# Half-height score products, splits of whole tiles and paired stores in a two-layer encoder on one core

## The chip, the cores and the metric

The kernel runs on one core of one Trainium2 chip. The metric is the device time of one execution in microseconds (us). The kernel before takes 1310.69 us, the median of 3 runs (1310.45 to 1311.05). About 0.2% (2.6 us) is the least difference that a measurement of this kernel can tell from none.

## The reference

Two encoder layers over 512 tokens of width 1024 in f32, and a final RMSNorm. Each layer adds three blocks to x: neighbourhood attention beside grouped-query attention with one output projection, attention over 256 memory tokens, and a gated feed-forward block with a convolution over positions. Only the grouped-query scores and the final norm matter here:

```
def gqa_block_attention(q, k, v):          # 8 query heads, 2 key heads, head width 64
    qb = q.reshape(b, nblk, Q_BLOCK, hkv, g, dh).transpose(1, 0, 2, 3, 4, 5)
    ...
        sc = jnp.einsum('bqkgd,bskd->bkgqs', qi, k, preferred_element_type=jnp.float32) * scale
        p = jax.nn.softmax(sc, axis=-1)
        return jnp.einsum('bkgqs,bskd->bqkgd', p.astype(v.dtype), v)
...
    return rms_norm(x, norm_final)
```

A query block is 128 tokens, and the sum over d in a score runs over 64 values.

## The kernel before

**Arithmetic.** Products are taken on TensorE in a rounded f32 type (F32R). To keep f32 accuracy each operand is split into a rounded part (hi) and what is left (lo): ACT casts hi, DVE or POOL subtracts lo. A full product is three products into one PSUM buffer, hi by hi, hi by lo, lo by hi (`mm3`, line 635).

**Layout.** x stands transposed in eight tiles xT of 128 rows of the model width by 512 tokens, one tile each (line 647). PSUM has buffers with three tags: mm (4), sc (2) and tr (2), each 128 x 512 f32.

**Grouped-query attention** (lines 1094 to 1269). `gqa_project_kv` and `gqa_project_q` project, normalise and turn k and q, and transpose them on TensorE, so that in the transposed tile the rows 0 to 63 belong to one key head and the rows 64 to 127 to the other. `split_k` (line 958) writes for each head j a tile gk[j] whose 128 rows hold that head's k twice: the head's 64 rows are cast and subtracted over 64 partitions, and a DMA (line 971) copies them to the other 64. `split_q` (line 976) writes q for head j with its hi on 64 rows and its lo on the other 64. With the rows stacked so, one product over 128 rows gives hi and lo of q at once, and `gqa_scores` (line 1206) needs two products for each head: q by hi of k and q by lo of k, both into that head's sc buffer. A unit u is one block of 128 queries and one pair of heads (j = 0, 1), so it has 4 products of 512 columns; 16 units a layer, 32 in all. Behind the products come the row maximum and its scaling on DVE, the exponential on ACT (which reads the sc buffer last), normalisation on POOL, transposes and the product with v.

**The order.** Nothing is issued where the code calls it. `Tape` records each call as a `Step` with a cost (`times`, line 125), and `plan` simulates the engines and chooses an order for each. On PE it takes, among up to 300 steps ahead, the first in the recorded order that can start within 60 ns of the earliest one; a step that opens a PSUM buffer can only start when a buffer of that tag is free. `play` (line 387) then issues all steps in the planned order. So every instruction in the profile has line 395, the call in `play`, and groups are told apart by tile names.

**The end** (`down_last`, line 1633). The last feed-forward product leaves 384 token columns in the layout of xT (output 0) and the last 128 tokens the other way round, as two halves of 512 model columns in two sc buffers (output 1). `squares` sums their squares on ACT and multiplies them by the norm's gains on DVE. The eight chunks of xT are scaled on DVE (five) and POOL (1, 4 and 6), and SP stores each by itself. Then 640 columns of the last 128 tokens are scaled by the root on DVE and stored by SP, 384 on ACT and stored from ACT's queue.

Of the kernel before, what the change touches and what calls it, by code (L numbers as in the profile page):

```python
# [11 lines left out]
F32 = mybir.dt.float32  # L12
F32R = mybir.dt.float32r
AF = mybir.ActivationFunctionType
ALU = mybir.AluOpType
# [4 lines left out]
P = 128  # L20
S = 512
D = 1024
# [4 lines left out]
KC = D // P  # L27
# [64 lines left out]
class Step:  # L92
# [32 lines left out]
    def times(self):  # L125

        n = max(columns(a) for a in (self.writes if self.engine == E_PE else self.reads + self.writes))
        if self.engine == E_PE:
            busy = max(110.0, (n + 32) / 2.4)
            if self.reads[0].dtype == F32 and self.name != "transpose" and "is_transpose" not in self.call[2]:  # L130
                busy = 222.0
            return busy, busy + 170.0
        narrow = min(a.ap[0][1] for a in self.writes) < P
        if self.engine == E_ACT:
            busy = 68.0 + 0.805 * n if any(tag_of(a.tensor) in IN_PSUM for a in self.reads) else 85.0 + 0.855 * n
            busy += 105.0 * (n > 1) * sum(columns(a) == 1 for a in self.reads) + 93.0 * (len(self.writes) > 1)
            return busy + 110.0 * narrow, busy + 105.0 + 100.0 * (len(self.writes) > 1)
        wide = sum(columns(a) > 16 for a in self.reads)
        if self.engine == E_DVE:
            if self.name == "tensor_tensor_reduce":  # L140
                return 382.0, 540.0
            busy = 64.0 + 1.05 * n
            if n <= 16:
                busy = 130.0
            elif self.name in ("tensor_scalar", "scalar_tensor_tensor"):
                busy = 120.0 + 1.05 * n if wide > 1 else 64.0 + 0.78 * n
            return busy, busy + 85.0
        if self.name in ("tensor_scalar", "tensor_copy"):
            busy = 245.0 + 0.82 * n
        else:  # L150
            busy = 480.0 + 145.0 * n if tag_of(self.reads[-1].tensor) == "mhalf" else 120.0 + 2.2 * n
        return busy, busy + 45.0
# [337 lines left out]
def encoder_kernel(ctx: ExitStack, tc: tile.TileContext, t: dict, out: list):  # L490
# [21 lines left out]
    def rtile(shape, dt=F32R):  # L512
        return rpool.tile([P, *shape], dt, tag="r", name=nm("r"), padded_shape=[P, *pad(shape)])
# [15 lines left out]
    def small(n):  # L529
        return spool.tile([P, n], F32, tag="s", name=nm("s"), padded_shape=[P, 16])  # L530
# [7 lines left out]
    f = lambda ap: ap.bitcast(F32)  # L538
# [105 lines left out]
            mm3(ps, wh[:, k, c], wl[:, k, c], *ops[k], k == first, k == last)  # L644


    xg0 = [xpool.tile([P, S + 1], F32, tag=f"x{c}", name=f"xT{c}") for c in range(KC)]
    xT = [x[:, 0:S] for x in xg0]
    par = cpool.tile([P, DEPTH, NPAR], F32, name="par")
    first = nc.const_aps.tensor(0.0, (P, P), F32)  # L650
# [240 lines left out]
    for l in range(DEPTH):  # L891
# [66 lines left out]
        def split_k(pm, kt, near):  # L958
            rows = [(slice(64 * j, 64 * j + 64), slice(64 - 64 * j, 128 - 64 * j)) for j in range(2)]
            for k, (r, o) in zip(kt, rows):  # L960
                ACT.copy(k[r, 0], pm[r])
                if near:
                    ACT.copy(k[o, 0], pm[r])
            for k, (r, o) in zip(kt, rows):
                DVE.tensor_sub(k[r, 1], pm[r], f(k[r, 0]))
                if near:
                    DVE.tensor_sub(k[o, 1], pm[r], f(k[r, 0]))

            def double():
                for k, (r, o) in zip(kt, rows):  # L970
                    SP.dma_start(f(k[o]), f(k[r]))

            if not near:
                double()
# [167 lines left out]
        def gqa_project_kv():  # L1142

            w = [get_w(("gkv", kh), AHEAD - kh) for kh in range(2)]
            keys, gv = [], rtile((NB, 2, P))
            for m in range(2):
                pm = ps_mm().rearrange("p (b c) -> p b c", b=2)
                for i in range(2):
                    bs = slice((2 * m + i) * P, (2 * m + i + 1) * P)
                    for k in range(KC):  # L1150
                        wh, wl = (v[:, k % 4, :] for v in w[k // 4])
                        mm3(pm[:, i], xg[k][0][:, bs], xg[k][1][:, bs], wh, wl, k == 0, k == KC - 1)
                        if k == 3 or k == KC - 1 and i == 0:
                            yield
                x = pm[:, :, 0:P].rearrange("p b (h d) -> p b h d", d=HD)
                b = slice(2 * m, 2 * m + 2)
                r = head_norm(x, 4, 1, b)
                for i in range(2):
                    gvt[2 * m + i] = gv[:, 2 * m + i]
                    split_psum(gvt[2 * m + i][:, :, 0:HD], gvt[2 * m + i][:, :, HD:P],  # L1160
                               pm[:, i, P:].rearrange("p (h d) -> p h d", d=HD), mix.rstd[:, 2 * m + i : 2 * m + i + 1])
                tk = tmp((2, P))
                turned(x, 4, 1, b, tk.rearrange("p b (h d) -> p b h d", d=HD))
                heads = tk.rearrange("p b (h d) -> p (b h) d", d=HD)
                POOL.tensor_mul(heads, heads, r.unsqueeze(2).to_broadcast([P, 4, HD]))
                keys.append(tk)
                yield

            def turn():
                tr = ps_t()  # L1170
                for b in range(NB):
                    PE.transpose(tr[:, b * P : (b + 1) * P], keys[b // 2][:, b % 2], ident)
                gk.extend(rtile((2, S)) for _ in range(2))
                split_k(tr, gk, False)

            late(2, turn)

# [18 lines left out]
        def gqa_turn_q(b, tq):  # L1196
            tr = ps_t()
            for i in range(4):
                PE.transpose(tr[:, i * P : (i + 1) * P], tq[:, i * P : (i + 1) * P], ident)
            gq[b] = rtile((2, 4, P))  # L1200
            split_q(tr.rearrange("p (i n) -> p i n", i=4), gq[b])


        ga, gpt = {}, {}
# [1 line left out]
        def gqa_scores(u):  # L1206
            i, b = divmod(u, NB)
            sc = [ps_s() for _ in range(2)]
            for j in range(2):
                for part in range(2):  # L1210
                    PE.matmul(sc[j], gq[b][:, j, i], gk[j][:, part], start=part == 0, stop=part == 1)
            nmx, sums = small(2), small(2)
            es = []
            for j in range(2):
                c, h = slice(j, j + 1), slice(2 * i + j, 2 * i + j + 1)
                DVE.tensor_reduce(nmx[:, c], sc[j], axis=AX.X, op=ALU.max, negate=True)
                DVE.tensor_scalar(nmx[:, c], nmx[:, c], gr[b][:, h], 1.0, op0=ALU.mult, op1=ALU.mult)
                e = tmp()
                ACT.activation(e, sc[j], AF.Exp, bias=nmx[:, c], scale=gr[b][:, h], accum_out=sums[:, c])
                es.append(e)  # L1220
            ga[u] = es, sums
# [411 lines left out]
        def down_last(j0, nj):  # L1633
# [41 lines left out]
            def squares(i):  # L1675
                sq = tmp()
                ACT.activation(sq, pms[i], AF.Square, accum_out=sums[:, i : i + 1])
                DVE.tensor_mul(y[:, i], pms[i], gains[:, 512 * i : 512 * i + 512])

            for i in range(2):  # L1680
                pms.append(ps_s())
                for c in range(4):
                    PE.matmul(pms[i][:, c * P : (c + 1) * P], xT[4 * i + c][:, tail], ident, start=c == 0, stop=False,
                              is_transpose=True)
                closing(i, range(2))
                if i == 0:
                    norm.stat()
                    closing(i, range(2, nj))
                    squares(i)
            part0, dev, rstd = small(1), small(1), small(1)  # L1690
            DVE.tensor_scalar(part0, sums[:, 0:1], 1.0 / D, EPS, op0=ALU.mult, op1=ALU.add)
            norm.spread()
            for k in range(KC):
                xk = xT[k][:, cs]
                if k in (1, 4, 6):
                    POOL.tensor_mul(xk, xk, norm.rep)
                else:
                    DVE.tensor_mul(xk, xk, norm.psum)
                SP.dma_start(out[0][k * P : (k + 1) * P, :], xk)
            closing(1, range(2, nj))  # L1700
            ACT.activation(small(1), sums[:, 0:1], AF.Sqrt)
            squares(1)
            ACT.activation(dev, sums[:, 1:2], AF.Sqrt, bias=part0, scale=1.0 / D)
            DVE.reciprocal(rstd, dev)
            yf = y.rearrange("p i n -> p (i n)")
            DVE.tensor_scalar(yf[:, :640], yf[:, :640], rstd, 1.0, op0=ALU.mult, op1=ALU.mult)
            SP.dma_start(out[1][:, 0:640], yf[:, :640])
            ACT.activation(yf[:, 640:], yf[:, 640:], AF.Copy, scale=rstd)
            ACT.dma_start(out[1][:, 640:D], yf[:, 640:])

        for n in range(NF):
            if n == 0:
# [164 lines left out]
```

## Time and profile before

| | us |
|---|---|
| median of 3 runs | 1310.69 |
| the profiled execution's own time | 1310.14 |
| its span, first to last instruction | 1308.0 |
| PE busy | 1299.9 |
| weight loads (PEld) busy, beside PE | 1121.9 |
| DVE / POOL / ACT busy | 1057.7 / 808.5 / 738.4 |

The granted TensorE clock has a mean of 0.998. In the rows of groups, "out<-in" are tile names, "128*128" behind PE is rows by columns of the array that the product uses, "128x512" the output, then the count; behind the bar stand busy us in total, mean ns of one, and the engine's idle time just before them with what ended it. A product's recorded duration reaches beyond the start of the next one, since products are pipelined; the spacing of starts is what each adds. The tiles in rows: r are operands in SBUF, sc, mm and tr are PSUM buffers, xT is x.

### The profile page before, as it was taken

What the parts mean: (1) busy time and instruction counts of PE and PEld (TensorE: products, weight loads), DVE (VectorE), ACT (ScalarE), POOL (GpSimd) and SP (SyncE); (2) the same over time, 40 slices, a digit from 0 to 9 for tenths busy, and PEclk for the clock granted to TensorE, in tenths of its full rate; (3) what the DMA queues carried; (4) which work ended last, traced back from release to release, by engine and by line L of the source; (5) the groups of instructions that cost most, each with busy time, mean ns of one, the idle gap of its engine ahead of it and who ended that gap; (6) DMA issues with size and microseconds to landing.
All of it is one profiled execution on the core that took longest, in us unless ns stands there. A gap on an engine that the chain in (4) does not pass through costs nothing.

```text
span 1308.0 us, 19584 instructions
## 1 busy us (share of the span) xinstructions
PE 1299.9 (99%) x6937; PEld 1121.9 (86%) x6937; DVE 1057.7 (81%) x2008; ACT 738.4 (56%) x1391; POOL 808.5 (62%) x607
## 2 busy tenths in 40 slices
PE   9999999999999999999999999999999999999997
PEld 8898888888888888888888988888888888888897
DVE  7679986766999998987545898956769999989865
ACT  7777686555445544544537767865645445444442
POOL 4465867627667677773726657774466667776651
PEclk9999999999999999999999999999999999999999
DMA  8742313313323333332365422233133333333321
GB/s 283 218 146 51 111 49 97 97 38 118 91 79 115 109 97 97 99 116 92 105 161 178 128 67 81 65 113 82 49 113 97 98 97 100 110 95 99 99 95 65
DMA packets 42673, 137.41 MB, mean 105 GB/s; under 512 B 5072, under 2 KB 8656, under 8 KB 42576
## 3 DMA queue, kind: packets, MB, share of 16 engines
q1 hardware_dynamic: 42144, 135.83, 34.6%
q8 instruction: 55, 0.90, 0.3%
q14 instruction: 42, 0.34, 0.1%
q10 hardware_dynamic: 432, 0.33, 0.1%
HBM read 126.18 MB, written 2.10 MB: 98 GB/s over the span
## 4 chain that ended last, share of the span: by engine, by line
PE 99%; DMA 1%; DVE 0%; ACT 0%; SPq 0%; issue 0%
PE mm L395 52%; PE sc L395 25%; PE tr L395 22%; DMA xT<-in_w 0%; DMA r<-in_w 0%; DVE xT L395 0%; ACT xg L395 0%; ACT r L395 0%; DVE tr L395 0%; DVE r L395 0%; ACT rep L395 0%; SPq L395 0%; ACT hi L395 0%; DVE s L395 0%
## 5 line engine op out<-in xcount | busy, mean ns | idle before, releaser
L395 POOL TENSOR_TENSOR lo<-raw,hi 128x512 fp32r<-128x512 f32 (+2 forms) x236 | 438.2, 1868 | 305.9 <-ACT hi L395 305.0
L395 ACT CAST hi<-raw 128x512 fp32r<-128x512 f32 (+2 forms) x276 | 219.9, 817 | 186.7 <-PE sc L395 70.8
L395 PE MATMUL mm<-r,hi 128*128 128x512 f32 (+2 forms) x928 | 247.1, 346 | 0.0
L395 PE MATMUL sc<-xg,hi 128*128 128x512 f32 (+1 forms) x740 | 229.0, 391 | 0.2 <-ACT hi L395 0.2
L395 PE MATMUL tr<-xg,hi 128*128 128x512 f32 x672 | 207.1, 389 | 0.0
L395 PEld LDWEIGHTS mm<-r,hi 128*128 128x128 f32 x928 | 163.2, 189 | 21.8
L395 PE MATMUL mm<-r,lo 128*128 128x256 f32 (+2 forms) x496 | 165.6, 334 | 0.0
L395 PEld LDWEIGHTS sc<-xg,hi 128*128 128x128 f32 x740 | 137.2, 189 | 27.3 <-ACT hi L395 0.6
L395 PE MATMUL mm<-r,r 128*128 128x256 f32 (+2 forms) x1040 | 158.4, 293 | 0.0
L395 PEld LDWEIGHTS tr<-xg,hi 128*128 128x128 f32 x672 | 126.0, 188 | 26.1
L395 PEld LDWEIGHTS mm<-r,r 128*128 128x128 f32 x1040 | 142.4, 191 | 2.7
L395 POOL TENSOR_TENSOR r<-t,r 128x512 fp32r<-128x512 f32 x80 | 117.9, 1478 | 42.5 <-ACT r L395 42.2
L395 PE MATMUL sc<-xg,lo 128*128 128x512 f32 (+1 forms) x370 | 143.5, 389 | 0.0
L395 ACT CAST r<-t 128x512 fp32r<-128x512 f32 (+1 forms) x164 | 94.4, 588 | 85.2 <-DVE t L395 68.7
L395 PE MATMUL tr<-xg,lo 128*128 128x512 f32 x336 | 130.7, 389 | 0.0
L395 DVE TENSOR_TENSOR xT<-xT,mm 128x256 f32<-128x256 f32 (+2 forms) x216 | 116.6, 559 | 15.8 <-PE mm L395 9.5
L395 PE MATMUL mm<-xg,hi 128*128 128x512 f32 (+1 forms) x386 | 121.7, 394 | 0.0
L395 DVE TENSOR_TENSOR t<-t,t 128x512 f32<-128x512 f32 (+2 forms) x110 | 116.5, 1079 | 5.5 <-ACT t L395 2.9
L395 PE MATMUL mm<-hi,xg 128*128 128x512 f32 (+1 forms) x384 | 108.5, 358 | 0.0
L395 POOL TENSOR_SCALAR t<-t,s 128x512 f32<-128x512 f32 (+1 forms) x112 | 67.2, 614 | 63.5 <-DVE s L395 57.6
L395 PEld LDWEIGHTS mm<-r,lo 128*128 128x128 f32 x496 | 93.9, 189 | 9.5
L395 DVE TENSOR_TENSOR r<-t,r 128x512 fp32r<-128x512 f32 (+1 forms) x84 | 81.6, 992 | 8.3 <-ACT r L395 7.6
(138 smaller groups left out, 2421.9 us busy)
## 6 DMA issues: line engine op xcount, KB each, us to landing
raw<-in_w SPq DMA_DIRECT2D x207, 512.0 KB, 3.7
r<-r SPq DMA_DIRECT2D x30, 256.0 KB, 3.6
r<-in_bias SPq DMA_DIRECT2D x16, 384.0 KB, 4.8
raw<-in_w SPq DMA_DIRECT2D x8, 384.0 KB, 3.0
r<-in_memT SPq DMA_DIRECT2D x4, 512.0 KB, 6.7
xT<-in_w SPq DMA_DIRECT2D x7, 256.5 KB, 4.5
out<-xT SPq DMA_DIRECT2D x8, 192.0 KB, 2.0
r<-in_w SPq DMA_DIRECT2D x9, 128.0 KB, 4.3
```

What stands on the lines that cost most here:

```text
L395: call(*args, **kwargs)
```

## The change

1. Scores: each head takes three products over its own 64 rows (hi by hi, hi by lo, lo by hi) in place of two over 128 rows, recorded alternately for the two heads, so that rows 0 to 63 and 64 to 127 follow each other.
2. q and k are split as the transpose left them: one cast and one subtraction over 128 partitions for both heads. The DMA that doubles k is gone, and so is one of the two k tiles of a layer.
3. The planner prices a product over fewer than 128 rows at half, plus 6 ns.
4. xT tiles are allocated in pairs, and the final store takes a pair: four stores of two chunks in place of eight of one.
5. The second half row is no longer multiplied by the gains ahead of the root; one DVE instruction multiplies it from PSUM by root and gains. The split of the last scaling goes from 640 and 384 columns to 512 and 512.

```diff
@@ Step.times
                 busy = 222.0
+            if self.reads[0].shape[0] < P:
+                return busy / 2 + 6.0, busy + 170.0
             return busy, busy + 170.0
@@ x's tiles
-    xg0 = [xpool.tile([P, S + 1], F32, tag=f"x{c}", name=f"xT{c}") for c in range(KC)]
+    xpair = [xpool.tile([P, 2, S + 1], F32, tag=f"x{c}", name=f"xT{c}") for c in range(KC // 2)]
+    xg0 = [xpair[c // 2][:, c % 2] for c in range(KC)]
@@ turn (k), gqa_turn_q
-                gk.extend(rtile((2, S)) for _ in range(2))
-                split_k(tr, gk, False)
+                gk.append(rtile((2, S)))
+                split_psum(gk[0][:, 0], gk[0][:, 1], tr)
...
-            split_q(tr.rearrange("p (i n) -> p i n", i=4), gq[b])
+            split_psum(gq[b][:, 0], gq[b][:, 1], tr.rearrange("p (i n) -> p i n", i=4))
@@ gqa_scores
-            for j in range(2):
-                for part in range(2):
-                    PE.matmul(sc[j], gq[b][:, j, i], gk[j][:, part], start=part == 0, stop=part == 1)
+            for n, (a, c) in enumerate(((0, 0), (0, 1), (1, 0))):
+                for j in range(2):
+                    r = slice(64 * j, 64 * j + 64)
+                    PE.matmul(sc[j], gq[b][r, a, i], gk[0][r, c], start=n == 0, stop=n == 2)
@@ down_last
                 ACT.activation(sq, pms[i], AF.Square, accum_out=sums[:, i : i + 1])
-                DVE.tensor_mul(y[:, i], pms[i], gains[:, 512 * i : 512 * i + 512])
...
                     squares(i)
+                    DVE.tensor_mul(y[:, 0], pms[0], gains[:, :512])
...
-                SP.dma_start(out[0][k * P : (k + 1) * P, :], xk)
+                if k % 2:
+                    SP.dma_start(out[0][(k - 1) * P : (k + 1) * P].rearrange("(i p) c -> p i c", p=P), xpair[k // 2][:, :, cs])
...
-            yf = y.rearrange("p i n -> p (i n)")
-            DVE.tensor_scalar(yf[:, :640], yf[:, :640], rstd, 1.0, op0=ALU.mult, op1=ALU.mult)
-            SP.dma_start(out[1][:, 0:640], yf[:, :640])
-            ACT.activation(yf[:, 640:], yf[:, 640:], AF.Copy, scale=rstd)
-            ACT.dma_start(out[1][:, 640:D], yf[:, 640:])
+            DVE.scalar_tensor_tensor(y[:, 1], pms[1], rstd, gains[:, 512:], op0=ALU.mult, op1=ALU.mult)
+            SP.dma_start(out[1][:, 512:], y[:, 1])
+            ACT.activation(y[:, 0], y[:, 0], AF.Copy, scale=rstd)
+            ACT.dma_start(out[1][:, :512], y[:, 0])
```

The planned order on PE, at the first two units of layer 0, in the kernel before (sc_401 and sc_402 are the buffers of the first unit's two heads, sc_411 and sc_412 those of the second's; r_350 and r_351 are the two heads' k):

```order
L395 MATMUL sc_401<-r_350,r_362 128x512 x2
L395 MATMUL sc_402<-r_351,r_362 128x512 x2
L395 MATMUL mm_410<-r_232,hi_391 128x512 x2
L395 MATMUL mm_410<-r_232,lo_392 128x512
L395 MATMUL mm_410<-r_284,hi_391 128x512 x2
L395 MATMUL mm_410<-r_284,lo_392 128x512
L395 MATMUL mm_410<-r_337,hi_391 128x512 x2
L395 MATMUL mm_410<-r_337,lo_392 128x512
L395 MATMUL mm_410<-r_372,hi_391 128x512 x2
L395 MATMUL mm_410<-r_372,lo_392 128x512
L395 MATMUL sc_411<-r_350,r_379 128x512 x2
L395 MATMUL mm_417<-r_232,hi_391 128x512
```

The same two units after the change (sc_396 and sc_397, then sc_406 and sc_407; r_346 holds both heads' k):

```order
L397 MATMUL sc_396<-r_346,r_357 128x512
L397 MATMUL sc_397<-r_346,r_357 128x512
L397 MATMUL sc_396<-r_346,r_357 128x512
L397 MATMUL sc_397<-r_346,r_357 128x512
L397 MATMUL sc_396<-r_346,r_357 128x512
L397 MATMUL sc_397<-r_346,r_357 128x512
L397 MATMUL mm_405<-r_228,hi_386 128x512 x2
...
L397 MATMUL sc_406<-r_346,r_374 128x512 x3
L397 MATMUL mm_412<-r_228,hi_386 128x512 x2
L397 MATMUL mm_412<-r_228,lo_387 128x512
L397 MATMUL sc_407<-r_346,r_374 128x512 x3
```

The first unit's six products alternate between the heads. The second unit's stand in two groups of three, one for each head, with three products of the output projection between. In all, 26 of the 32 units stand like the second, 3 like the first, and 3 in between.

At the end of the program, SP's last instructions before the change (xT_76 to xT_83 are the eight chunks, r_2389 the last 128 tokens):

```order
L395 DMA out<-xT_76 128x384
L395 DMA out<-xT_77 128x384
L395 DMA out<-xT_78 128x384
L395 DMA out<-xT_79 128x384
L395 DMA out<-xT_80 128x384
L395 DMA out<-xT_81 128x384
L395 DMA out<-xT_82 128x384
L395 DMA out<-xT_83 128x384
L395 DMA out<-r_2389 128x640
```

And after it (xT_76 to xT_79 are the four pairs):

```order
L397 DMA out<-xT_76 128x2x384
L397 DMA out<-xT_77 128x2x384
L397 DMA out<-xT_78 128x2x384
L397 DMA out<-xT_79 128x2x384
L397 DMA out<-r_2383 128x512
```

Nine stores became five. The first store of before waits for DVE alone, which scales chunk 0; the first of after waits for DVE and for POOL, which scales chunk 1.

## The prediction

> **What bounds the kernel now.** I read the page first: busy time by engine, then the chain of work that ended last. After it come the waits of PE alone, and pieces of the chain in order of time.
>
> ```profile
> span 1308.0 us, 19584 instructions
> PE 1299.9 (99%) x6937; PEld 1121.9 (86%) x6937; DVE 1057.7 (81%) x2008; ACT 738.4 (56%) x1391; POOL 808.5 (62%) x607
> ...
> PE 99%; DMA 1%; DVE 0%; ACT 0%; SPq 0%; issue 0%
> ```
>
> ```profile
> PE tr L395 <- PEq L1869: 0.8, 1, 0.8
> PE sc L395 <- ACT hi L395: 0.2, 1, 0.2
> ```
>
> ```profile
> 465.57 5.47 PE sc L395 x24
> ...
> 663.85 21.88 PE mm L395 x96
> ```
>
> PE is busy for 1299.9 of 1308.0 us, the chain is PE for 99%, and in the whole span PE waits 1.0 us for anybody. So time is what PE's instructions cost, one behind the other, and a few us at the end. An instruction's price on this chain is not its recorded duration but its spacing: 5.47 us for 24 products of 512 columns is 228 ns each, and 21.88 us for 96 is 228 ns again. The stage that the change rewrites must be looked at by itself, so I asked for busy time by engine from the first to the last group of grouped-query scores in each layer (columns: length, then PE, weight loads, DVE, ACT, POOL).
>
> ```profile
> 135.90:202.00 66.10, 66.10 (x361) 55.65 (x360) 60.73 (x132) 52.31 (x113) 50.21 (x53) 1.00 0.25 73
> 781.00:858.00 77.00, 76.95 (x420) 64.51 (x419) 69.30 (x149) 60.78 (x130) 55.91 (x59) 1.00 0.24 73
> ```
>
> PE is busy for 66.10 of 66.10 us and for 76.95 of 77.00; DVE comes next with 60.73 and 69.30. Here too PE alone decides, at a granted clock of 1.00.
>
> **Scores: what a product of 64 rows costs.** There are 32 units (2 layers of 16), one each for a query block and a pair of heads. Before, a unit has 4 products over 128 rows: 4 x 228 = 912 ns. After, it has 6 over 64 rows. The trace has none over 64 rows; the nearest rows are the groups of products with shapes kept apart (last two numbers ahead of the bar's end: busy us, mean ns).
>
> ```profile
> L395 PE MATMUL sc<-xg,hi 128*128 128x512 f32 x732 | 226.4, 390 | 0.2 <-ACT hi L395 0.2
> ...
> L395 PE MATMUL sc<-r,r 128*128 128x256 f32 x224 | 33.7, 285 | 0.0
> ...
> L395 PE MATMUL mm<-r,r 128*128 128x384 f32 x96 | 17.3, 334 | 0.0
> ```
>
> From 256 to 384 to 512 columns the mean goes 285, 334, 390 ns: the price follows the columns that stream through, about 0.4 ns each. Rows are 128 in every row of this trace, so their effect is not shown. Bounds for one 64-row product of 512 columns: half, 114 ns, if price went with the share of the array in use, and 228 ns if it goes with columns alone. I take 228, since columns explain all three rows. Then the half array that is left unused pays only if the other head's product runs in it at the same time. For such a pair the bounds are 228 ns (wholly beside) and 456 ns (one behind the other); I take 228, as two products over separate rows and separate PSUM buffers share neither.
>
> So all hangs on which products stand next to each other, and there the order of the change decides. Its rows above show the first unit alternating between the two heads (sc_396, sc_397), six products in a row. The next shows three products of one head (sc_406 x3), three products over 128 rows, and then three of the other head (sc_407 x3). I went through all 32 units in the order:
>
> - 3 units alternate cleanly. Each costs 3 x 228 instead of 4 x 228 ns: 3 x -0.23 = -0.7 us.
> - 3 are broken in part (one product alone, then five alternating, twice; and once two of each head, then one of each). Each fills 4 slots of 228 ns, as before: 0.
> - 26 have all three products of one head, then 1 to 10 products of other work over 128 rows, then all three of the other. Three products on the same 64 rows cannot stand beside each other, and the next on PE needs all rows. Each costs 6 x 228 instead of 4 x 228 ns, +0.456 us: 26 x 0.456 = +11.9 us.
>
> The sum is **+11.2 us**, all of it on PE, which the chain runs through. The Trainium skill, "TensorE: Matmul & The Clock Gate", Part 3 (The mechanism), states that matmuls in different row groups start about 4 ns apart, and that matmuls start and end strictly in program order; by the first the pair costs 232 ns, and by the second a head's three products cannot move across the others to find a partner. No run yet shows the first.
>
> **Splits of q and k.** With the head's two halves left where the transpose puts them, 20 casts and 20 subtractions over 64 partitions become 10 and 10 over 128, and 4 copies of k (r<-r) leave SP's queue.
>
> ```profile
> L395 DVE TENSOR_TENSOR r<-tr,r 128x512 fp32r<-128x512 f32 x48 | 32.4, 685 | 10.8 <-ACT r L395 10.5
> ...
> L395 DVE TENSOR_TENSOR r<-tr,r 64x512 fp32r<-64x512 f32 x20 | 13.8, 689 | 0.7 <-issue 0.2
> L395 ACT CAST r<-tr 64x512 fp32r<-64x512 f32 x20 | 11.6, 579 | 6.9 <-PE tr L395 6.6
> ```
>
> Sixty-four or 128 partitions cost the same (689 and 685 ns), so DVE saves 10 x 0.69 = 6.9 us and ACT 10 x 0.58 = 5.8 us. On the path that is worth nothing: PE hides it, since it never waits for a split in the two stages. If that cover went (PE faster by 7.3 us over two stages, the best case), DVE would still have 60.73 - 3.4 = 57.3 us of work in a stage of 62.4. Between 0 and -0.2 us, the one wait for ACT that there is; I take 0. The planner lays out the whole program anew, but instruction counts by kind are otherwise the same, and it counts on scores that are done sooner than I expect, so what waits for PE has more time than planned: 0, up to +1 us if one hand-over goes wrong.
>
> **The end.** Stores of x's rows now go in pairs, and the last half row is multiplied straight from PSUM. I read the last 9 us in order of time, each engine by itself, and then the DMA rate (last column, GB/s) in short stretches.
>
> ```profile
> 1299.49 2.41 DVE L395 TENSOR_TENSOR xT<-xT,tr 128x384 f32<-128x384 f32 x5 [0.54 <-ACT rep L395]
> 1299.53 1.01 POOL L395 TENSOR_TENSOR xT<-xT,rep 128x384 f32<-128x384 f32 x1 [2.97 <-ACT rep L395]
> ...
> 1300.07 0.34 SPq L395 DMA_DIRECT2D out<-xT  x1
> ...
> 1300.58 0.85 SPq L395 DMA_DIRECT2D out<-xT  x2
> ...
> 1301.82 0.69 DVE L395 TENSOR_TENSOR r<-sc,r 128x512 f32<-128x512 f32 x1
> ...
> 1304.02 0.60 SPq L395 DMA_DIRECT2D out<-r  x1
> ```
>
> ```profile
> 1300.60:1300.80 0.20, 0.20 (x2) 0.00 (x0) 0.20 (x1) 0.00 (x0) 0.20 (x1) 1.00 0.00 0
> 1300.80:1301.00 0.20, 0.11 (x1) 0.00 (x0) 0.20 (x2) 0.06 (x1) 0.20 (x1) 1.00 0.36 131
> 1301.00:1301.20 0.20, 0.00 (x0) 0.00 (x0) 0.20 (x1) 0.20 (x1) 0.20 (x1) 1.00 1.04 376
> ...
> 1306.25:1306.50 0.25, 0.00 (x0) 0.00 (x0) 0.00 (x0) 0.00 (x0) 0.00 (x0) 0.50 0.98 369
> 1306.50:1306.75 0.25, 0.00 (x0) 0.00 (x0) 0.00 (x0) 0.00 (x0) 0.00 (x0) 0.50 0.11 31
> ```
>
> From 1300.9 to 1306.5 us the DMA engines are full, at about 375 GB/s. The removed DVE multiply (0.69 us) and the last store, which now comes some 1 us sooner on SP, stand beside this and bring nothing. What sets the end is when the first byte leaves and how many there are. The bytes are the same (8 x 192 + 320 + 192 KB before, 4 x 384 + 2 x 256 after). The first store left at 1300.07, when DVE had its chunk; after, it needs POOL's chunk too, which ends at 1299.53 + 1.01 = 1300.54, and in the trace the second store, which waits for that, leaves at 1300.58. So everything starts 0.5 us later: **+0.5 us**, with 0 if larger stores move faster and +0.7 if they take longer to issue.
>
> **Sum.** The profiled execution took 1310.14 us, and + 11.2 + 0.5 makes 1321.8. The median of the three runs, 1310.69, lies 0.55 above that execution; I forecast against it: **1322.4 us**.
>
> **Rivals.**
>
> *Half price (faster).* A 64-row product costs its half whatever stands next to it, 114 ns. Then a unit costs 684 instead of 912 ns: 32 x -0.228 = -7.3, +0.5 at the end: 1303.9 us. It decides wherever the price of a product lies under 912 / 6 = 152 ns. For it: no row here varies the number of rows, and in the new order each head's three products share their moving and stationary buffers. Against it: columns alone explain the means at 256, 384 and 512. Chance 0.11. A price close to 152 would give no change: 0.03.
>
> *Every change of rows empties the array.* The recorded 390 ns of a product, less its spacing of 228, leaves about 161 ns in which a product is still under way while the next streams. If PE must be empty before it goes from 128 rows to 64 or back, each change costs up to that. The 32 units stand in 60 unbroken runs of 64-row products, thus 120 changes: up to 120 x 0.161 = +19.3 us, 1341.7 us. The Trainium skill, "TensorEngine Tiling (Array Packing)", Key Properties, says that a change of tiling mode drains the TensorE, while another tile in the same mode does not; all groups here are 128*128, so nothing in this trace shows it. For it: 60 runs is an order that would suffer most. Against it speaks the nearest change of kind that PE makes now, from transposes to products and back, in order of time.
>
> ```profile
> 142.72 0.60 PE L395 MATMUL tr<-ident,t 128*128 128x128 f32 x4
> 143.07 0.48 PE L395 MATMUL mm<-r,hi 128*128 128x512 f32 x1
> 143.39 0.60 PE L395 MATMUL tr<-ident,t 128*128 128x128 f32 x4
> 143.74 1.18 PE L395 MATMUL sc<-r,r 128*128 128x512 f32 x4
> 144.76 0.39 PE L395 MATMUL mm<-r,hi 128*128 128x512 f32 x1
> ```
>
> Eight transposes and five products take 2.04 us from 142.72 to 144.76; less 5 x 0.228 that is 112 ns for a transpose of 128 columns, and no room for four changes at 0.16. I give a cost that is well visible (over 8 us) 0.20, and let smaller ones stand within the forecast, whose own range is 1318 to 1330: 0.62.
>
> *Weight loads come to light.*
>
> ```profile
> L395 PEld LDWEIGHTS sc<-r,r 128*128 128x128 f32 x376 | 57.6, 189 | 5.8 <-DMA r<-r 0.2
> ```
>
> If loads onto the same 64 rows did not run beside products there, up to 189 ns for each of the 192 products, 36 us more: 1358 us. Against it, PEld is busy for 1121.9 us beside PE's 1299.9, all of it on the same rows. Chance 0.04.
>
> **How the numbers follow.** Forecast 0.62, emptied array 0.20, loads 0.04, half price 0.11, no change 0.03. The range takes in the first two: 1316 to 1344. About 0.2% (2.6 us) is what a measurement of this kernel can tell from no change; so faster 0.11, same 0.03, slower 0.86.
>
> **What the changed profile would show.** Products marked by 64 rows: 192 of them, spaced by 228 ns within a run of three, and two that start within a few ns in the 3 clean units. Stages of about 66.1 + 5.0 and 77.0 + 6.2 us (12 and 14 whole units at 0.456, less 2 and 1 x 0.228). A spacing near 114 in runs of three makes me wrong towards faster; a gap at each first product of a run, or behind its last, makes the second rival right. At the end, a first store near 1300.6 on the old clock, and DMA full for 5.6 us behind it. PE waiting for DVE or ACT in these stages would say that the new plan, not the products, is at work.

## The result, and the profile after

The changed kernel takes 1346.21 us (median of 4 runs, 1344.84 to 1347.60), the kernel before beside it 1310.87 (4 runs, 1310.45 to 1312.35): a ratio of 1.027, 95% interval 1.0256 to 1.0281. It is 35.3 us slower. Slower was forecast; the time lies 2.2 us above the range.

The page after, and the waits of PE:

```profile
span 1344.5 us, 19676 instructions
PE 1335.2 (99%) x7001; PEld 1125.6 (84%) x7001; DVE 1051.5 (78%) x1997; ACT 733.0 (55%) x1381; POOL 807.2 (60%) x607
```

```profile
PE tr L397 <- PEq L1873: 0.8, 1, 0.8
PE sc L397 <- DMA r<-r: 0.4, 1, 0.4
PE sc L397 <- DVE xg L397: 0.2, 1, 0.2
```

PE still waits for nobody (1.4 us in all) and is busy 35.3 us longer; DVE and ACT are busy 6.2 and 5.4 us less; the splits were to save them 6.9 and 5.8. To divide the loss between the stream on PE and the end, take the last eleven products of both programs (line 397 is line 395 of before), the store of the first chunk, and the span. Before:

```profile
1298.16 2.75 PE L395 MATMUL sc<-r,r 128*128 128x512 f32 x11
1298.98 0.48 ACT L395 COPY rep<-tr 128x384 f32<-128x384 f32 x1 [0.62 <-DVE tr L395]
1300.07 3.86 SPq L395 DMA_DIRECT2D out<-xT  x8
```

After:

```profile
1333.98 2.77 PE L397 MATMUL sc<-r,r 128*128 128x512 f32 x11
1334.80 0.48 ACT L397 COPY rep<-tr 128x384 f32<-128x384 f32 x1 [0.61 <-DVE tr L397]
1336.40 2.59 SPq L397 DMA_DIRECT2D out<-xT  x4
1338.78 0.35 ACTq L397 DMA_DIRECT2D out<-r  x1
1339.08 0.90 SPq L397 DMA_DIRECT2D out<-r  x1
```

The last products start 35.82 us later; from there to the end of the span it was 9.84 us and is 10.52: +0.7 at the end. Of the 35.8 us, 11.2 were forecast. The other 24.6 can be seen where the units stand. This is PE in order of time at the first two units (start, length, then the group):

```profile
135.95 0.60 PE L397 MATMUL tr<-ident,t 128*128 128x128 f32 x4
136.47 0.96 PE L397 MATMUL sc<-r,r 64*128 64x512 f32 x6
137.37 0.73 PE L397 MATMUL mm<-r,hi 128*128 128x512 f32 x2
137.94 0.39 PE L397 MATMUL mm<-r,lo 128*128 128x512 f32 x1
...
139.98 0.39 PE L397 MATMUL mm<-r,lo 128*128 128x512 f32 x1
140.30 0.96 PE L397 MATMUL sc<-r,r 64*128 64x512 f32 x3
141.19 0.73 PE L397 MATMUL mm<-r,hi 128*128 128x512 f32 x2
141.76 0.39 PE L397 MATMUL mm<-r,lo 128*128 128x512 f32 x1
```

Six products that alternate between the heads last as long (0.96) as three of one head: pairs do run side by side. But from 139.98 to 141.76 six products start, each 228 ns, 1.37 us together, and 1.78 us pass: the run of three costs 0.41 us more than its products. The 192 products stand in 60 unbroken runs (52 of three, the others of one, five or six). If each pays the same, that is 60 x 0.41 = 24.6 us, all that was missing. The weight loads of the same place show what happens there:

```profile
139.76 0.19 PEld L397 LDWEIGHTS mm<-r,lo 128*128 128x128 f32 x1
140.30 0.52 PEld L397 LDWEIGHTS sc<-r,r 64*128 64x128 f32 x3 [0.35 <-ACT t L397]
141.19 0.30 PEld L397 LDWEIGHTS mm<-r,hi 128*128 128x128 f32 x2 [0.37 <-issue]
```

Within work of one kind a load runs ahead, beside the product before it (the load at 139.76 is for the product at 139.98). At a change from 128 rows to 64, and at the change back, the load starts only 0.32 us after the last product's start (139.98 to 140.30, 140.87 to 141.19), some 0.09 later than the next product would have started. The next product's start is recorded at the same moment as its load, and the second product of a run starts 0.335 us after the first instead of 0.228; we read this as a first product that is held up by its own load, which costs 0.11. Together 0.20 us a change, twice a run. The name in the brackets misleads: the trace puts the first gap down to ACT, whose first exponential over the first unit had ended at 139.30, and the second to "issue". But at all 58 changes from a run back to a product over 128 rows the gap is 0.315 to 0.324 us, whatever the profile names.

### The profile page after: what moved, and what is told of

It is laid out like the page before. It is cut to its first block, busy times and chain, and to the rows that moved or that the text cites. A ratio compares the mean times of both kernels' runs of the same rounds, so it can differ in the third digit from the quotient of the medians.

```text
span 1344.5 us, 19676 instructions
## 1 busy us (share of the span) xinstructions
PE 1335.2 (99%) x7001; PEld 1125.6 (84%) x7001; DVE 1051.5 (78%) x1997; ACT 733.0 (55%) x1381; POOL 807.2 (60%) x607
## 4 chain that ended last, share of the span: by engine, by line
PE 98%; DVE 1%; DMA 1%; ACT 0%; issue 0%; DVEq 0%
PE mm L397 51%; PE sc L397 26%; PE tr L397 21%; DMA r<-r 1%; ACT t L397 0%; DVE t L397 0%; ACT r L397 0%; DVE sc L397 0%; DVE s L397 0%; DVE r L397 0%; ACT hi L397 0%; DVE mm L397 0%; DVE xT L397 0%; DVE xg L397 0%; ACT s L397 0%
## 5 line engine op out<-in xcount | busy, mean ns | idle before, releaser
L397 PE MATMUL mm<-r,hi 128*128 128x512 f32 (+2 forms) x928 | 250.8, 349 | 0.0
L397 PE MATMUL sc<-r,r 128*128 128x256 f32 (+2 forms) x440 | 96.7, 353 | 0.4 <-DMA r<-r 0.4
```

What stands on the lines that cost most here:

```text
L397: call(*args, **kwargs)
```

## The experiments

Three theories went in. **A**: each change of PE between 128 and 64 rows costs 0.20 us, and products cost a slot of 228 ns each, shared by two on different halves. **B**: 64-row products are dear by themselves. **C**: the new order of the program costs the time. The kernel before, beside these runs, took 1310.73 us for the first four, 1311.18 for the next three and 1310.54 for the last two.

**All rows, same order.** The price stays at half by a flag, so that the planned order on PE is the same, product for product.

```diff
-                    r = slice(64 * j, 64 * j + 64)
-                    PE.matmul(sc[j], gq[b][r, a, i], gk[0][r, c], start=n == 0, stop=n == 2)
+                    PE.matmul(sc[j], gq[b][:, a, i], gk[0][:, c], start=n == 0, stop=n == 2)
```

> The changed kernel with its six products a unit taken over all 128 rows of the tiles in place of 64, in the same order of instructions on PE (so the scores sum both heads, and the output is not the reference's). It changes nothing but the number of rows. Theory A (each change of PE between 128 and 64 rows costs about 0.20 us, 120 of them): the changes are gone, and 192 products cost 228 ns where 128 did, +14.6 us, with +0.6 at the end: 1326 us. Theory B (every 64-row product is dear by itself, 0.11 us more than one of 128 rows, because its weight load comes to light): 1326 us too. Theory C (the new order, made with a price of half a product, costs the time): 1340 us or more, since the order stays.

1325.68 us, a ratio of 1.0115 (1.010 to 1.013). The order alone costs nothing, C is out: with it and without changes of rows the sum of products (+14.6) and the end (+0.6) account for the time. The changed kernel, with the same products in the same order on PE, takes 20.5 us more although 16 pairs save it a slot each (3.6 us). That is 24.2 us for 120 changes, 0.20 each; theory B could still claim them for the 192 products. The same place as above:

```profile
139.84 0.39 PE L400 MATMUL mm<-r,lo 128*128 128x512 f32 x1
140.07 0.84 PE L400 MATMUL sc<-r,r 128*128 128x512 f32 x3
140.75 0.62 PE L400 MATMUL mm<-r,hi 128*128 128x512 f32 x2
141.20 0.39 PE L400 MATMUL mm<-r,lo 128*128 128x512 f32 x1
```

The same six products take 1.36 us from 139.84 to 141.20, against 1.78 with 64 rows.

**Pairs without anything between.** The six products are one step for the planner, with a price of 1089 ns. (The planner's rule for free buffers is extended, since such a step opens two.)

```diff
-            for n, (a, c) in enumerate(((0, 0), (0, 1), (1, 0))):
-                for j in range(2):
-                    r = slice(64 * j, 64 * j + 64)
-                    PE.matmul(sc[j], gq[b][r, a, i], gk[0][r, c], start=n == 0, stop=n == 2)
+            def scores(sc0, accum_out, qh, ql, kh, kl):
+                for n, j in [(n, j) for n in range(3) for j in range(2)]:
+                    r = slice(64 * j, 64 * j + 64)
+                    q, k = ((qh, kh), (qh, kl), (ql, kh))[n]
+                    nc.tensor.matmul((sc0, accum_out)[j], q[r], k[r], start=n == 0, stop=n == 2)
+            tape.take(E_PE, "scores", scores, (sc[0],), {"accum_out": sc[1], ...})
```

> The changed kernel with the six products of a unit issued as one block that alternates between the heads, so that none of the planned work comes between them: 32 runs of 64-row products in place of 60, all of them paired. Theory A: each unit costs 3 slots of 228 ns plus two changes, 1.089 us, against 0.912 before: 32 x 0.177 = +5.7, +0.6 at the end: 1317 us, slower than before although every product has its partner. Theory B: six dear products a unit, paired or not, about 1346 us if they don't run side by side, and 1315 if they do (3 x 0.335 us a unit), which the spacings in the trace would tell apart. Full gain without a cost of changes: 1304 us.

1317.78 us, a ratio of 1.0052 (1.0036 to 1.0069). As A says: with every product paired the change is still slower than before. 7.05 us over before, less 0.6 at the end, plus the 7.3 that pairing saves, are 13.7 us for 64 changes: 0.215 each. Not all of that is the changes: in the profile PE now waits 3.1 us for others in place of 1.0.

```profile
PE 1305.3 (99%) x7001; PEld 1111.6 (84%) x7001; DVE 1053.3 (80%) x1997; ACT 731.3 (56%) x1381; POOL 807.7 (61%) x607
```

```profile
PE mm L400 <- DVE xg L400: 1.6, 2, 0.8
```

By PE's busy time alone, 1305.3 against 1299.9, and the 7.3 saved, a change costs 0.20.

**Head by head.** The same step, with the order of the six changed (and its price for the planner raised to 1545 ns).

```diff
-                for n, j in [(n, j) for n in range(3) for j in range(2)]:
+                for n, j in [(n, j) for j in range(2) for n in range(3)]:
```

> The same block of six, but three products of one head and then three of the other. Two changes a unit as in the block that alternates, 64 in all, but only the third and the fourth product can stand side by side. Theory A: 5 slots of 228 ns plus 0.405, 1.545 us a unit, +20.3 +0.6: 1332 us; 6 slots, 1339 us, if two neighbours don't pair unless the order alternates throughout. Theory B: 1346 us. It also shows whether going from rows 0-63 to rows 64-127 costs anything; by theory A it does not, since both are 64-row products.

1318.50 us (1.0059, 1.0044 to 1.0074). All expectations missed: it is as fast as the order that alternates. The first unit of it on PE:

```profile
136.66 0.97 PE L1219 MATMUL sc<-r,r 64*128 64x512 f32 x6
137.56 0.50 PE L400 MATMUL mm<-r,hi 128*128 128x512 f32 x1
```

Six products in 0.97 us, and 0.90 to the next work, are three slots and the changes, so the fourth to sixth started beside the first to third. Products on different halves do not keep to the program's order. The Trainium skill, "TensorE: Matmul & The Clock Gate", Part 3 (The mechanism), says that matmuls start and end strictly in program order; this run does not agree, since in that order at most one pair of these six could run side by side.

**The scores and splits of before, with the changed end and layout of x.**

```diff
-                gk.append(rtile((2, S)))
-                split_psum(gk[0][:, 0], gk[0][:, 1], tr)
+                gk.extend(rtile((2, S)) for _ in range(2))
+                split_k(tr, gk, False)
...
-            split_psum(gq[b][:, 0], gq[b][:, 1], tr.rearrange("p (i n) -> p i n", i=4))
+            split_q(tr.rearrange("p (i n) -> p i n", i=4), gq[b])
```

(and the four products of before in `gqa_scores`).

> The changed kernel with scores and the splits of q and k put back as before (two products of 128 rows a head); the paired stores, the last half row and the planner's price for short products (which then meets none) stay. Theory A: only the end is left, +0.6 us by the first store that waits for POOL too: 1311.5 us. If the layout of x in pairs or the new end cost more than that, it shows here: 1313 us or more.

1310.78 us, a ratio of 0.9999 (0.999 to 1.0009): the end makes no difference that this measurement sees. The profile sees it: this span too is 1308.0 us, and

```profile
1297.50 2.77 PE L397 MATMUL sc<-r,r 128*128 128x512 f32 x11
1298.31 0.48 ACT L397 COPY rep<-tr 128x384 f32<-128x384 f32 x1 [0.61 <-DVE tr L397]
1299.91 2.60 SPq L397 DMA_DIRECT2D out<-xT  x4
```

from these products to its end it takes 10.50 us, as after the change, and 9.84 before. The first store leaves 1.60 us behind ACT's copy in place of 1.09. In this execution PE's last products came 0.66 us sooner than before, which hides it; why they did is open.

**The cost of a change by itself.** Two kernels with the same nine products a unit: the six of the alternating step, and three whose sums are overwritten. They differ in the place of the one over 128 rows, and in the planner's price for the step (1545 and 1950 ns), so that 329 of the 7097 products stand in another order. `short(n)` issues the n-th pair, `whole()` one product over 128 rows. Control:

```diff
+                whole()
+                short(0, True)
                 for n in range(3):
                     short(n)
```

> The block of six that alternates, with three redundant products ahead of it in each unit, whose sums the next product overwrites: one over 128 rows and then one pair over 64. No change of rows is added, since the product over 128 rows stands behind work over 128 rows. This is the control for the next kernel. Theory A (a cost for each change of rows): 2 slots of 228 ns more a unit, 32 x 0.456 = 14.6 us over the 1317.8 us of the block alone: 1332.4 us. Theory B (64-row products are dear by themselves): 32 x (0.228 + 0.335) = 18 us, 1336 us.

1330.67 us (1.0149, 1.0133 to 1.0164). And the other:

```diff
-                whole()
                 short(0, True)
+                whole()
                 for n in range(3):
                     short(n)
```

> The same nine products a unit as in the control, but the one over 128 rows stands between the redundant pair and the six: the same work, and two more changes of rows in each unit, 64 in all. It measures the disputed cost by itself. Theory A, at 0.20 to 0.215 us a change: 13 to 14 us more than the control, 1346 us. Theory B and every theory without a cost for changes: the control's time, within 1 us.

1344.59 us (1.0254, 1.024 to 1.0268). The first unit in the control, and then in the other:

```profile
135.62 0.60 PE L400 MATMUL tr<-ident,t 128*128 128x128 f32 x4
135.97 0.47 PE L1223 MATMUL sc<-r,r 128*128 128x512 f32 x1
136.38 1.20 PE L1220 MATMUL sc<-r,r 64*128 64x512 f32 x8
137.50 0.73 PE L400 MATMUL mm<-r,hi 128*128 128x512 f32 x2
```

```profile
135.80 0.60 PE L400 MATMUL tr<-ident,t 128*128 128x128 f32 x4
136.33 0.50 PE L1220 MATMUL sc<-r,r 64*128 64x512 f32 x2
136.76 0.49 PE L1223 MATMUL sc<-r,r 128*128 128x512 f32 x1
137.18 0.97 PE L1220 MATMUL sc<-r,r 64*128 64x512 f32 x6
138.08 0.73 PE L400 MATMUL mm<-r,hi 128*128 128x512 f32 x2
```

From the first transpose to the product behind the unit it is 1.88 us in the control and 2.28 in the other, 0.40 for two changes; the medians differ by 13.9 us for 64, 0.22 each (0.20 to 0.23 between the extremes of the runs). Of these, 1.1 us are waits of PE for others that only the second kernel has; by PE's busy time (1331.8 less 1319.3; the control's page first) a change costs 0.20:

```profile
PE 1319.3 (99%) x7097; PEld 1123.5 (85%) x7097; DVE 1051.1 (79%) x1997; ACT 730.8 (55%) x1381; POOL 805.8 (61%) x607
PE 1331.8 (99%) x7097; PEld 1124.7 (84%) x7097; DVE 1049.1 (78%) x1997; ACT 731.0 (54%) x1381; POOL 806.7 (60%) x607
```

The control came out 1.7 us under theory A and 5 under B, and B gave no difference between the two: B is out.

**Two units in a run.** If a change has a price of its own, longer runs should pay for it. This is the kernel before, with its own end and the changed splits.

```diff
+            sc = [ps_s(), ps_s(), ps_mm(), ps_mm()]     # two query blocks
+            def scores(sc0, out, out2, out3, q0, q1, k):
+                tiles = (sc0, out), (out2, out3)
+                for n, (a, c) in enumerate(((0, 0), (0, 1), (1, 0))):
+                    for to, q in zip(tiles, (q0, q1)):
+                        for j in range(2):
+                            r = slice(64 * j, 64 * j + 64)
+                            nc.tensor.matmul(to[j], q[r, a], k[r, c], start=n == 0, stop=n == 2)
...
```

> The kernel before with its own end, and the scores of two units (two query blocks) as one run of twelve 64-row products in four PSUM buffers (two of tag sc, two of tag mm), with the changed splits of q and k. Theory A: 16 runs cost 6 x 0.228 + 0.405 = 1.773 us each, 28.4 us, against 32 x 0.912 = 29.2 before: 0.8 us less, 1309.9 us, unless the two mm buffers that the scores now hold make PE wait, which would show as waits of PE for DVE or ACT in the score stages. Theory B: 16 x 6 x 0.335 = 32.2, 1313.7 us.

1319.28 us (1.0059, 1.0046 to 1.0072). The run costs what was expected: twelve products from 136.24, and the next work at 137.84, 1.60 us (plus 0.2 around it). The gain of 0.8 us is lost elsewhere:

```profile
PE tr L398 <- DVE s L398: 4.0, 4, 1.7
PE mm L398 <- DVE t L398: 1.4, 2, 0.9
```

```profile
197.00:200.00 3.00, 2.17 (x14) 1.23 (x13) 2.60 (x5) 1.35 (x4) 3.00 (x4) 1.00 0.42 147
200.00:203.00 3.00, 1.22 (x5) 0.92 (x6) 2.97 (x10) 2.51 (x7) 1.39 (x2) 0.78 0.30 56
203.00:206.00 3.00, 3.00 (x10) 2.31 (x9) 1.98 (x7) 1.69 (x5) 2.39 (x4) 0.50 0.37 149
206.00:209.00 3.00, 3.00 (x10) 2.44 (x9) 1.25 (x2) 1.82 (x4) 0.51 (x1) 0.58 0.00 0
209.00:212.00 3.00, 3.00 (x19) 2.56 (x18) 1.52 (x4) 1.86 (x4) 1.28 (x1) 1.00 0.00 0
```

At the end of the first score stage PE sits idle for 2.6 of 6 us (197 to 203). Behind that the granted clock (third number from the end) falls to 0.50, while PE is busy again, and comes back to 1.00 from 209 on. The second layer shows the same: idle for 2.2 of 8 us (850 to 858), with a clock of 0.50 from 854 on. In this execution, the slowest of the five, PE waits 7.5 us in all in place of 1.0, and is busy 5.3 us longer in place of 0.8 shorter. So the longer runs brought waits for DVE, and a lower clock followed the idle time. What of it comes from the two buffers taken from the other products, and what from the softmax of two units that starts at once, was not separated.

**How far out of order.** The head-by-head step with each head's three products repeated.

```diff
-                for n, j in [(n, j) for j in range(2) for n in range(3)]:
+                for n, j in [(n, j) for j in range(2) for _ in range(2) for n in range(3)]:
```

> The block that goes head by head, with each head's three products issued twice (the first sums are overwritten): six of one head, then six of the other. It asks how far ahead of its turn a product on the other 64 rows can start. If it reaches six products ahead: 6 slots of 228 ns and two changes, 1.773 us a unit, 0.684 more than the block of six: 32 x 0.684 over 1318.5 = 1340 us. If PE kept to the program's order but for neighbours: 11 slots, 2.913 us a unit, 1377 us.

1355.69 us (one run). Then four times, twelve of each head:

> The same with four times three: twelve products of one head, then twelve of the other. If a product on the other rows reaches twelve ahead: 12 slots, 3.141 us a unit, 32 x 2.052 over 1318.5 = 1384 us. If it reaches about six, the first six or so of the twelve run alone: some 18 slots, 1428 us.

1443.64 us (one run). Neither of the reaches named beforehand fits. Two stretches of the twelve-deep unit (start of the group, then the time to the end of its last product; each answer lists what was under way in its stretch):

```profile
135.53 2.12 PE L1219 MATMUL sc<-r,r 64*128 64x512 f32 x8
```

```profile
137.26 0.73 PE L1219 MATMUL sc<-r,r 64*128 64x512 f32 x3
```

The first eight last 2.12 us: they run alone. The third product of the second row is the first of the other head; it starts in the trace at 137.50, 7 ns behind the ninth of the first head, thus beside the one that stands four places ahead of it. From there four of each head run side by side, and eight are left over: 20 slots, 4.56 us and 0.2 for the first load and the wait at the end, of the 4.91 from the run's start to the next work. In the six-deep run the other head starts beside the third, four places ahead again: 8 slots, 1.82 + 0.2, of 2.16 us. In both some 0.14 us are left over. Most of that is the other head's own first load: its second product starts 0.335 us behind its first, not 0.228.

## Why the prediction was wrong

- **What bounds the kernel.** Right: PE's stream sets the time, before and after. The end and the layout of x were worth nothing that a run can see (0.9999 with the scores of before), and the run over all rows, which has the changed splits, comes out within 0.3 us of a sum that puts them at nothing.
- **Price of a 64-row product, and of a pair.** Right. A slot is some 0.23 us with 64 rows or 128; a pair takes one slot (0.96 us for three pairs, 0.96 for three singles).
- **26 of 32 units find no partner.** Right, +11.9 us: in the trace all 52 of their runs are three products one behind the other. The reason given for it, strict order, was too strong: with nothing between them a head's products run beside the other head's. In none of these units did they pass the products over 128 rows that stood between. Of the 3 units "broken in part", the one with two of each head is in fact fully paired: 0.90 us to the next work, as the clean ones.
- **Changes of rows: the step that failed.** The sum has no term for them; the rival "every change of rows empties the array" had a chance of 0.20. They cost 0.20 to 0.22 us, 120 times: 24 to 26 us. The gap at the first product of a run and behind its last, which the prediction named as that rival's sign, is there. Two errors are in that step. The evidence against the rival was a change from transposes to products, but both stand in the trace as 128*128; that row could not speak about a change of rows. And the bound of 0.161 us was made from the tail of a recorded product alone; the weight load that can no longer run ahead adds 0.11 us to a wait of 0.09. So even the rival, at 1341.7, was short by 4.5 us. The Trainium skill says that a change of tiling mode drains the engine ("TensorEngine Tiling (Array Packing)", Key Properties). The trace agrees in that PE waits at a change of rows and not between the halves; that the array is empty by then is not shown: the next product starts at 140.30, ahead of the last one's recorded end (139.98 + 0.39 = 140.37).
- **Weight loads.** The rival of 189 ns a product did not come: within a run on the same rows the spacing stays at 0.23 us, and only the first load of a run comes to light.
- **Half price.** Did not come: the second and third product of a run are 0.23 us apart, not 0.114.
- **The end.** Right in the trace: +0.7 us for +0.5, with the first store at 1300.58 on the old clock, as forecast for 1300.6. The medians with the changed end alone show no difference.

The direction was right, but of the 35 us only 11 come from the reason that was given. With 60 runs at 0.41 us the same sum gives 1322.4 + 24.6 + 0.2 for the end, less 0.2 for the unit that pairs after all: 1347.0, against 1346.2 measured. The 0.41 is read from the changed kernel itself; the two kernels of nine products give it independently, 0.40.

## What to carry to other kernels

Packing products into halves of the array pays by the run, not by the product: here a pair saves 114 ns a product and a run costs 0.41 us for going in and out, so a run must save two slots of 228 ns before it can gain anything, and one unit saves one. Two units in one run would just gain by this count (0.8 us over the whole kernel), but that kernel lost far more to waits. Before packing, look in the built order at what the scheduler puts between; a scheduler that prices a product without its neighbours will break the runs. And a row of the profile is evidence only about what varies in it: a trace with one array shape says nothing about changing the shape.

## What the runs showed of the hardware

- A change of PE between 128*128 and 64*128 products costs 0.20 to 0.22 us, whether after products of 512 columns (load 0.32 us behind the last start) or after transposes of 128 columns (0.20 us behind, where the next transpose would have come at 0.11).
- Three products on one half of the rows and then three on the other take as long as the six in turns, 0.90 us to the next work. Products on the other half start beside one that stands up to four places ahead of them. Where the first half is already running, in the twelve-deep run, the other half's first load still costs 0.11 us.
- After PE was idle for 2.6 of 6 us, the granted clock was 0.50 to 0.58 for the next 6 us of full work, and then 1.00 again.
